# A second feed-forward product by seven half-block products on one Trainium2 core, with its sums kept on chip

## The chip, the cores and the metric

The kernel runs on one core of a Trainium2 chip. The metric is the device time of one execution in microseconds. TensorE (PE in the rows) multiplies into PSUM banks; VectorE (DVE), ScalarE (ACT) and GpSimd (POOL) work on tiles in SBUF and PSUM; SyncE (SP) issues most of the transfers. Each engine works through its own list in order and waits where an operand of an instruction isn't ready.

## The reference, cut to what matters

The program is one layer of a diffusion backbone. The change lies in its last part, the feed-forward block, for 128 context tokens and 1024 latent ones (1152 in all, nine tiles of 128; tile 0 is the context), with 1024 columns and 4096 hidden columns, in float32:

```python
u = layer_norm(x) * (1.0 + scale2) + shift2
hid = jnp.square(jax.nn.relu(u @ lw['w_fc'] + lw['b_fc']))
x = layer_norm(ALPHA * x + gate2 * (hid @ lw['w_proj'] + lw['b_proj']), lw['ln_g'][1], lw['ln_b'][1])
```

`gate2` is a row for the context tokens and one for the latent ones (`g2c`, `g2l` in the kernel); the kernel makes both from `w_ada` in `ada_rest`.

## The kernel before, in words

Every float32 operand is split into a high and a low part (`split`, L67 on ScalarE for the high part and L68 on VectorE or GpSimd for the low one), and each product is three matmuls (`mm3`, L111 to L113).

*First product* (`ffn1`, hidden = w_fc by u). The 4096 hidden columns are 16 pairs p of 128-column blocks. p = 0 and 1 are plain products. From p = 2 on each p is computed by Strassen's scheme in Winograd's form: a 2 by 2 split of the weights and of the tokens, seven products where the plain way has eight, with sums of weight parts (`prep`, tiles `S`) and of token parts (`sums`, tiles `Th` and `Tl`) made beforehand. A p is 14 steps (seven products, two token halves) of 12 matmuls 128x288. `need(n)` lets the preparation of weights run ahead. Each p ends with one store of its tile H (L1095), which VectorE has squared (L1260).

*Second product* (`ffn2`, hidden by w_proj) is plain. It runs over eight blocks b of four hidden tiles each, and in each over nine token tiles t: 24 matmuls 128x512 per tile, 1728 in all. VectorE adds each result onto `acc[t]` (L1341). `ahead(b + 1)` loads and splits the next block's hidden tiles (`lo`, `hi`) and weights (`ws`, `w`) meanwhile, and `ada_rest` makes the last columns of the gates between the tiles of blocks 0 to 5. In block 6 `residual(t)` multiplies by the gate (L1347, GpSimd) and adds ALPHA times `x2` (L1349, VectorE). In block 7 `stage_a` and `stage_c` finish each token tile: two halves of gate, addition and statistics on VectorE (L1378 to L1380), a small group (L1381, L130, L1384), normalising on ScalarE, `lng` and `lnb` on GpSimd (L1386, L1395). The last tile closes on VectorE (L1389, L1390).

## Time and profile before

| | |
|---|---|
| time, median of 3 runs | 2298.06 us (2292.59 to 2298.08) |
| the profiled execution, its own time | 2287.31 us |
| its span, first to last instruction | 2285.5 us |
| mean granted TensorE clock | 0.978 |
| PE busy | 94% of the span |
| DVE, ACT, POOL busy | 58%, 40%, 29% |

Busy shares are means over the whole span. A granted clock of 1.0 is TensorE's upper level (2.4 GHz), 0.5 the lower (1.2 GHz). A row of an instruction gives its start, its duration, its engine and line, what it writes and reads, and in brackets the engine's idle time before it and what ended that.

### The profile page before, as it was taken

The numbers are of one execution on the slowest core, as the hardware profiler recorded it, in microseconds if no ns is written. First come the engines' busy times: TensorE is split into PE (matmuls) and PEld (weight loads), VectorE is DVE, ScalarE is ACT, GpSimd is POOL, SyncE is SP. The second block draws the span as 40 slices with busy tenths as digits, with TensorE's granted clock in tenths as the row PEclk, the third lists the DMA queues.
The fourth block names the chain that finished last, engine by engine and source line by source line (L and its number), as shares of the span: only waits on it lengthen the run. The fifth ranks groups of instructions, "written<-read, shape, count | busy, mean of one in ns | idle before, by whom it ended". The sixth has DMA issues, their size and how long they took to land. (4 is left out here: it accounts for less than half of the span.)

```text
span 2285.5 us, 31722 instructions
## 1 busy us (share of the span) xinstructions
PE 2150.3 (94%) x12723; PEld 2021.9 (88%) x12723; DVE 1333.9 (58%) x2154; ACT 922.3 (40%) x1496; POOL 666.7 (29%) x367
## 2 busy tenths in 40 slices
PE   7988998999999899999999999969999979999996
PEld 4888998999999899999899998869999968888885
DVE  4464775676574555888734457764544436543378
ACT  5354424414424425787723224644444431121112
POOL 1402212412311312332302024353434302321176
PEclk9999999999999999999999999989999979999998
DMA  6121241133122121111432333442223253322442
GB/s 269 37 71 39 68 148 47 64 110 104 54 87 87 52 78 47 47 47 38 152 103 94 122 118 128 133 148 88 109 80 118 79 188 129 111 88 79 138 138 83
DMA packets 96755, 223.84 MB, mean 98 GB/s; under 512 B 20132, under 2 KB 48420, under 8 KB 93536
## 3 DMA queue, kind: packets, MB, share of 16 engines
q1 hardware_dynamic: 75008, 204.44, 26.5%
q10 hardware_dynamic: 21600, 17.38, 2.3%
q8 instruction: 99, 1.62, 0.3%
q14 instruction: 48, 0.39, 0.1%
HBM read 171.70 MB, written 50.09 MB: 97 GB/s over the span
## 5 line engine op out<-in xcount | busy, mean ns | idle before, releaser
L111 PE MATMUL pj<-hi,w 128*128 128x384 f32 (+1 forms) x2120 | 704.0, 332 | 22.4 <-ACT w L67 17.6
L112 PE MATMUL pj<-lo,w 128*128 128x384 f32 (+1 forms) x2120 | 701.2, 331 | 11.6 <-DVE lo L68 7.5
L113 PE MATMUL pj<-hi,w 128*128 128x384 f32 (+1 forms) x2120 | 700.8, 331 | 0.5 <-POOL w L68 0.5
L111 PEld LDWEIGHTS pj<-hi,w 128*128 128x128 f32 x2120 | 402.8, 190 | 24.5 <-ACT w L67 17.9
L112 PEld LDWEIGHTS pj<-lo,w 128*128 128x128 f32 x2120 | 402.7, 190 | 12.5 <-DVE lo L68 8.1
L113 PEld LDWEIGHTS pj<-hi,w 128*128 128x128 f32 x2120 | 402.3, 190 | 0.8 <-POOL w L68 0.8
L68 POOL TENSOR_TENSOR w<-ws,w 128x1024 fp32r<-128x1024 f32 (+1 forms) x91 | 187.5, 2064 | 559.1 <-ACT w L67 492.7
L67 ACT ACTIVATE w<-ws 128x1024 fp32r<-128x1024 f32 (+1 forms) x175 | 159.2, 915 | 384.8 <-DMA ws<-in_w_pr 241.3
L111 PE MATMUL pps<-w,hi 128*128 128x512 f32 x576 | 225.8, 392 | 15.4 <-ACT w L67 15.4
L112 PE MATMUL pps<-w,hi 128*128 128x512 f32 x576 | 226.0, 392 | 1.5 <-DVE w L68 1.5
L113 PE MATMUL pps<-w,lo 128*128 128x512 f32 x576 | 225.6, 392 | 0.0
L68 DVE TENSOR_TENSOR w<-ws,w 128x1024 fp32r<-128x1024 f32 (+1 forms) x84 | 104.9, 1255 | 107.3 <-ACT w L67 107.2
L1341 DVE TENSOR_TENSOR acc<-pps,acc 128x512 f32<-128x512 f32 x108 | 73.7, 691 | 146.6 <-PE pps L113 146.5
L111 PEld LDWEIGHTS pps<-w,hi 128*128 128x128 f32 x576 | 108.9, 189 | 39.4 <-ACT w L67 16.6
L111 PE MATMUL pj<-Th,w 128*128 128x288 f32 x448 | 132.7, 296 | 9.7 <-ACT e L1246 9.7
L113 PE MATMUL pj<-Th,w 128*128 128x288 f32 x448 | 132.0, 295 | 0.0
L112 PE MATMUL pj<-Tl,w 128*128 128x288 f32 x448 | 131.9, 294 | 0.0
L112 PEld LDWEIGHTS pps<-w,hi 128*128 128x128 f32 x576 | 109.0, 189 | 25.0 <-DVE w L68 2.4
L113 PEld LDWEIGHTS pps<-w,lo 128*128 128x128 f32 x576 | 109.1, 189 | 22.5
L716 POOL TENSOR_TENSOR CS<-Cst,CS 128x516 fp32r<-128x516 f32 x56 | 74.4, 1328 | 183.9 <-ACT CS L715 178.3
L464 POOL PARTITION_ALL_REDUCE aacc<-aacc x16 | 56.0, 3545 | 196.3 <-DVE aacc L463 170.3
L111 PEld LDWEIGHTS pj<-Th,w 128*128 128x128 f32 x448 | 84.0, 188 | 11.5 <-ACT e L1246 11.5
(313 smaller groups left out, 4055.1 us busy)
## 6 DMA issues: line engine op xcount, KB each, us to landing
ws<-in_w_in SPq DMA_DIRECT2D x56, 512.0 KB, 4.1
h<-Hf SPq DMA_DIRECT2D x16, 1152.0 KB, 5.1
lo<-h SPq DMA_DIRECT2D x32, 576.0 KB, 3.6
aw<-in_w_ada SPq DMA_DIRECT2D x64, 256.0 KB, 3.6
ws<-in_w_fc SPq DMA_DIRECT2D x32, 512.0 KB, 3.3
ws<-in_w_pr SPq DMA_DIRECT2D x32, 512.0 KB, 4.2
gm<-gs ACTq DMA_DIRECT2D x48, 192.0 KB, 1.9
gmr<-gm SPq DMA_DIRECT2D x16, 576.0 KB
```

The source lines that it names most:

```text
L67: self.nc.scalar.activation(hi, x, AF.Copy)
L68: (eng or self.nc.vector).tensor_tensor(lo, x, hi.bitcast(F), OP.subtract)
L111: mm(out, lhsT=ah, rhs=bh, start=first, stop=False, skip_group_check=onto)
L112: mm(out, lhsT=ah, rhs=bl, start=False, stop=False, skip_group_check=onto)
L113: mm(out, lhsT=al, rhs=bh, start=False, stop=last, skip_group_check=onto)
L464: nc.gpsimd.partition_all_reduce(acc[j], acc[j], channels=128, reduce_op=ReduceOp.add)
L716: nc.gpsimd.tensor_tensor(CS[d][1], Cst[d], CS[d][0].bitcast(F), OP.subtract)
L1341: nc.vector.tensor_tensor(acc[t][:, s], pss[n], (acc[t] if b else bp)[:, s], OP.add)
```

## The change

The second product is made by the same seven-product scheme for the eight latent tiles. Tokens and hidden columns are split in two; `KINDS` names the products by the weight part (B11, B21, B22) or sum of parts (T1 to T4) that they use. B12 is for the context alone, which stays plain. The hidden pairs fall in five blocks (`F2`) of 4, 4, 2, 4 and 2 pairs. Each product runs for four token slots j, 16 pairs by 4 slots by 7 products by 3 matmuls, 1344, and the context has 192: 1536 matmuls. Results per product are added up on chip in `Cj` and `Xj` over blocks 0 to 3; `combine` then puts them together at the end of block 3, with the gate and the residual (`residual`, L1501 and L1502). Block 4 adds its products on top in PSUM and finishes the tokens (`do`, `finish`, `norm`); before its first product `until(b, "B22")` issues all that is left of its preparation.

The hidden sums that the scheme needs are made in the first product. `store(p)` became a generator with four GpSimd sums of 512 columns and six transfers, which is run at the even steps of later p's. The token sums all come ahead of the first weight split, and `load(2)` stands a weight block earlier. The first product has 6 PSUM banks instead of 8. The last two columns of `ada_rest` move to the two branches of the mixer.

```diff
-            self.h_d = [self.dram.tile([128, 2, T], F, name=f"h{i}") for i in range(16)]
+            self.h_d = self.dram.tile([128, 7, 16, 512], F, name="h_d")
+            self.hc_d = self.dram.tile([128, 16, 2, 128], F, name="hc_d")
...
+        self.sides.append(self.ada_rest(p, range(6, 8), 1))
...
-        self.npj = 8
+        self.npj = 6
...
         def store(p, H):
-            nc.sync.dma_start(self.h_d[p], H)
...
+            a, b = (H[:, :, 128 + 512 * k:640 + 512 * k] for k in range(2))
+            to = lambda i, n=1: self.h_d[:, i:i + n, p, :]
+            t = lambda: pe.tile([128, 512], F, name="S", tag="S", bufs=5)
+            g = nc.gpsimd
+            s1, s2, s4 = t(), t(), t()
+            g.tensor_tensor(s1, b[:, 0], b[:, 1], OP.add)
             yield
...
+            g.tensor_tensor(s2, s1, a[:, 0], OP.subtract)
+            nc.sync.dma_start(self.hc_d[:, p], H[:, :, 0:128])
+            nc.sync.dma_start(to(0, 2), a)
+            yield
+            g.tensor_tensor(b[:, 0], a[:, 0], b[:, 0], OP.subtract)
+            nc.sync.dma_start(to(4)[:, 0], s1)
+            yield
+            g.tensor_tensor(s4, a[:, 1], s2, OP.subtract)
+            nc.sync.dma_start(to(5)[:, 0], s2)
+            yield
+            nc.sync.dma_start(to(2, 2), b)
+            yield
+            nc.sync.dma_start(to(6)[:, 0], s4)
+            yield
...
+                if p and i:
+                    load(2)
...
+                    if p and i:
+                        need(c)
...
+                self.f2_start()
+            if i in (6, 9, 12):
+                self.f2_ahead(i // 3 - 2)
...
+                elif stores and next(stores[0], stores) is stores:
+                    stores.pop(0)
...
+    F2 = [(0, 4), (4, 4), (8, 2), (10, 4), (14, 2)]
+    KINDS = ["B11", "B12", "T1", "T2", "T3", "B21", "T4", "B22"]
+    ROW = {"B11": 0, "T1": 4, "T2": 5, "T3": 2, "B21": 1, "T4": 3, "B22": 6}
...
+        def ahead():
+            for b in range(NB):
+                g = self.F2[b][1]
+                load_raw(b)
+                self.f2_load(b, None)
+                split = [lambda i=i: self.f2_split(b, None, i) for i in range(2)]
+                for kind in self.KINDS:
+                    n = H_KINDS.index(kind) if kind != "B12" else None
+                    if n is not None and (b or n):
+                        while not unit_free(b, n):
+                            yield
+                        if b or n > 1:
+                            self.f2_load(b, n)
+                        split += [lambda i=i: self.f2_split(b, n, i, g_ if i or kind in ("T1", "T2") else v) for i in range(2)]
+                    for i in range(g // 2):
+                        if (b, kind, i) not in self.wts:
+                            own = b == NB - 1 and kind in ("B21", "T4", "B22")
+                            while (own and "w" not in late) or (not own and tiles[0] >= tiles[1] + 5):
+                                yield
+                            self.w2, self.nw2 = (late["w"], 3) if own else (pw if tiles[0] % 5 == 4 else None, 1)
+                            tiles[0] += not own
+                            self.f2_weight(b, kind, [source(b, kind, 2 * i + j) for j in range(2)], i, [g_, v])
+                            yield
+                    while split:
+                        split.pop(0)()
+                        yield
+                    done.add((b, kind))
+        work = ahead()
...
+        def until(b, kind):
+            n = 0
+            while (b, kind) not in done:
+                next(work, None)
+                n += 1
+                assert n < 100
...
+        acc = {"B11": lambda j: Xj[j][:, 0], "T1": lambda j: Cj[j][:, 3], "T2": lambda j: Xj[j][:, 1],
+               "T3": lambda j: Xj[j][:, 2], "B21": lambda j: Cj[j][:, 0], "T4": lambda j: Cj[j][:, 2],
+               "B22": lambda j: Cj[j][:, 1]}
+        half = {"T1": 1, "B21": 0, "T4": 0}
...
+        def residual(t):
+            y = tile_of(t)
+            x2 = big("x2", ("r21", "r30", "r31")[t % 3])
+            nc.sync.dma_start(x2, self.x2_d[t])
+            g_.tensor_tensor(y, y, rows["g2l" if t else "g2c"], OP.mult)
+            v.scalar_tensor_tensor(y, x2, ALPHA, y, OP.mult, OP.add)
...
+        def combine(kind):
+            for j in range(4):
+                C, X = Cj[j], Xj[j]
+                add = lambda e, o, x: e.tensor_tensor(o, o, x, OP.add)
+                if kind == "T2":
+                    add(v, X[:, 1], X[:, 0])
+                elif kind == "T3":
+                    add(g_, X[:, 2], X[:, 1])
+                    add(g_, X[:, 1], C[:, 3])
+                    add(v, C[:, 3], X[:, 2])
+                elif kind == "B21":
+                    add(g_, C[:, 0], X[:, 0])
+                elif kind == "T4":
+                    add(g_, C[:, 2], X[:, 2])
+                    residual(5 + j)
+                elif kind == "B22":
+                    add(v, C[:, 1], X[:, 1])
...
+        for b in range(NB - 1):
+            for q, kind in enumerate(self.KINDS):
+                until(b, kind)
+                if kind in ("B11", "B12", "B21", "B22"):
...
+                if kind != "B12":
+                    for j in range(4):
+                        ps = bank()
+                        product(b, kind, j, ps)
+                        o = acc[kind](j)
+                        if b:
+                            v.tensor_tensor(o, ps, o, OP.add)
...
+                    used.add(7 * b + H_KINDS.index(kind))
+                tiles[1] += self.F2[b][1] // 2
+                if b == NB - 2:
+                    if kind == "T3":
+                        row("g2l", "r20", self.mod_d[3][1])
+                        row("g2c", "bp", self.mod_d[3][0])
+                    combine(kind)
+                    if kind == "B22":
+                        residual(0)
+        px.close()
+        late["w"] = self.pool(st, "w3")
+        b = NB - 1
+        until(b, "B22")
+        row("lng", "r00", I["ln_g"][1:2, :])
+        row("lnb", "r01", I["ln_b"][1:2, :])
...
+        def keep(i, j):
+            if i == 1:
+                x = big("e", ("r21", "r30")[j % 2])
+                ev[1, j], ev[2, j] = x[:, 0:512], x[:, 512:D]
+            elif i == 3:
+                x = big("e", ("r31", "r10")[j % 2])
+                ev[3, j], ev[4, j] = x[:, 0:512], x[:, 512:D]
+            nc.scalar.activation(ev[i, j], A[j], AF.Copy)
...
+        def do(P, j):
+            if P == 1:
+                A[j] = bank()
+                product(b, "B11", j, A[j])
+                keep(1, j)
+            elif P == 5:
...
+            elif P == 6:
+                product(b, "T2", j, A[j], False)
+                keep(2, j)
+            elif P == 7:
+                product(b, "T3", j, A[j], False)
+                keep(3, j)
...
+                t = ev[4, j]
+                v.tensor_tensor(t, Cb[j], ev[3, j], OP.add)
+                v.tensor_tensor(t, t, rows["g2l"][:, 512:D], OP.mult)
+                y = tile_of(5 + j)[:, 512:D]
+                v.tensor_tensor(y, y, t, OP.add)
...
+            elif P == 4:
+                product(b, "T4", j, A[j], False)
+                finish(5 + j, 0, A[j])
...
+        seq = [(1, 0), (5, 0), (6, 0)]
+        for j in range(4):
+            n = j + 1
+            seq += [(1, n), (7, j), (5, n), (2, j), (4, j), (3, j), (6, n)] if n < 4 else \
+                   ["B11", (7, j), "B12", (2, j), (4, j), (3, j), "B21", "B22"]
+        for x in seq:
```

SP's order between the two products, before: the last store of H, the bias row, two weights, four hidden tiles.

```order
L1095 DMA h_119<-Hf 128x2304 [waits DMAHW7_49,DVE_49]
L1310 DMA bp<-in_b_pr 128x1024 [waits DMAHW0_49,PE_49]
L1296 DMA ws<-in_w_pr 128x1024 [waits DMAHW5_49,DMAHW1_49]
L1296 DMA ws<-in_w_pr 128x1024 [waits DMAHW6_49,DMAHW2_49]
L1287 DMA lo<-h_106 128x1152 [waits DMAHW3_49,PE_49]
L1287 DMA lo<-h_106 128x1152 [waits DMAHW4_49,PE_49]
L1287 DMA lo<-h_107 128x1152 [waits PE_49] x2
```

After: the last sum's store, the bias row, the eight weights of block 0 (`raw`), then the context's tile (`hc_d`) and the next product's tokens. 

```order
L1119 DMA h_d<-S 128x512 [waits DMAHW5_49,Pool_49]
L1524 DMA bp<-in_b_pr 128x1024 [waits DMAHW6_49,PE_49]
L1387 DMA raw<-in_w_pr 128x1024 [waits DMAHW7_49]
L1387 DMA raw<-in_w_pr 128x1024 [waits DMAHW0_49]
L1387 DMA raw<-in_w_pr 128x1024 [waits DMAHW1_49]
L1387 DMA raw<-in_w_pr 128x1024 [waits DMAHW2_49]
L1387 DMA raw<-in_w_pr 128x1024 [waits DMAHW3_49]
L1387 DMA raw<-in_w_pr 128x1024 [waits DMAHW4_49]
L1387 DMA raw<-in_w_pr 128x1024 [waits DMAHW5_49]
L1387 DMA raw<-in_w_pr 128x1024 [waits DMAHW6_49]
L1332 DMA lo<-hc_d 128x1024 [waits DMAHW7_49,PE_49]
L1335 DMA lo<-h_d 128x2048 [waits DMAHW0_49]
```

The first product's own tokens and half weights stand further up, but what the first matmuls (the context's) need has moved behind the stores of the sums and all eight weights.

GpSimd's order at the end of block 6, before: gate multiplications (L1347) and splits of the next block's weights, then the first tokens' `lng` (L1386).

```order
L68 TENSOR_TENSOR w<-ws,w 128x1024 [waits DMAHW0_49,Activation_49]
L1347 TENSOR_TENSOR acc_17279<-acc_17279,g2l 128x1024 [waits DVE_49]
L1347 TENSOR_TENSOR acc_17280<-acc_17280,g2l 128x1024 [waits DVE_49]
L68 TENSOR_TENSOR w<-ws,w 128x1024 [waits DMAHW3_49,Activation_49]
L1347 TENSOR_TENSOR acc_17281<-acc_17281,g2l 128x1024 [waits DVE_49]
L1347 TENSOR_TENSOR acc_17282<-acc_17282,g2l 128x1024 [waits DVE_49]
L1386 TENSOR_TENSOR acc_17274<-acc_17274,lng 128x1024 [waits Activation_49]
L1386 TENSOR_TENSOR acc_17275<-acc_17275,lng 128x1024 [waits Activation_49]
```

After, at the end of block 3: the four multiplications of `combine("B22")` (L1501) and the context's, then the first of the instructions that prepare block 4 (L68 splits, L1397 and L1399 differences of weights).

```order
L1501 TENSOR_TENSOR C_17536<-C_17536,g2l 128x1024 [waits DVE_49]
L1501 TENSOR_TENSOR C_17537<-C_17537,g2l 128x1024 [waits DVE_49]
L1501 TENSOR_TENSOR C_17538<-C_17538,g2l 128x1024 [waits DVE_49]
L1501 TENSOR_TENSOR C_17539<-C_17539,g2l 128x1024 [waits DVE_49]
L1501 TENSOR_TENSOR ctx<-ctx,g2c 128x1024 [waits DMAHW1_49]
L68 TENSOR_TENSOR w<-raw,w 128x512 [waits Activation_49] x2
L68 TENSOR_TENSOR lo<-lo,hi 128x512 [waits DMAHW2_49,Activation_49]
L68 TENSOR_TENSOR lo<-lo,hi 128x512 [waits Activation_49]
L68 TENSOR_TENSOR w<-raw,w 128x512 [waits Activation_49]
L68 TENSOR_TENSOR lo<-lo,hi 128x512 [waits DMAHW3_49,Activation_49]
L68 TENSOR_TENSOR lo<-lo,hi 128x512 [waits Activation_49]
L1397 TENSOR_TENSOR raw<-raw 128x512 [waits DMAHW4_49,Pool_49]
```

The multiplications no longer alternate with splits: they stand in one piece, each waiting for VectorE, and the 19 instructions of block 4's preparation have moved behind them.

VectorE's order in block 6, before: evictions (L1341) and residuals (L1349).

```order
L1341 TENSOR_TENSOR acc_17276<-pps,acc_17276 128x512 [waits PE_49] x2
L68 TENSOR_TENSOR lo<-lo,hi 128x1152 [waits DMAHW5_49,Activation_49]
L1349 SCALAR_TENSOR_TENSOR acc_17275<-x_19166,acc_17275 128x1024 [waits DMAHW3_49,Pool_49]
L1341 TENSOR_TENSOR acc_17277<-pps,acc_17277 128x512 [waits PE_49] x2
L1349 SCALAR_TENSOR_TENSOR acc_17276<-x_19200,acc_17276 128x1024 [waits DMAHW4_49,Pool_49]
L1341 TENSOR_TENSOR acc_17278<-pps,acc_17278 128x512 [waits PE_49] x2
L68 TENSOR_TENSOR lo<-lo,hi 128x1152 [waits DMAHW6_49,Activation_49]
L1349 SCALAR_TENSOR_TENSOR acc_17277<-x_19237,acc_17277 128x1024 [waits DMAHW6_49,Pool_49]
L1341 TENSOR_TENSOR acc_17279<-pps,acc_17279 128x512 [waits PE_49] x2
L1349 SCALAR_TENSOR_TENSOR acc_17278<-x_19271,acc_17278 128x1024 [waits DMAHW7_49,Pool_49]
```

After, behind the last eviction of block 3: additions (L1508) and residuals (L1502), then block 4's weights.

```order
L1508 TENSOR_TENSOR C_17536<-C_17536,X_17551 128x512 [waits DVE_49]
L1502 SCALAR_TENSOR_TENSOR C_17536<-x_19744,C_17536 128x1024 [waits DMAHW5_49,Pool_49]
L1508 TENSOR_TENSOR C_17537<-C_17537,X_17552 128x512
L1502 SCALAR_TENSOR_TENSOR C_17537<-x_19749,C_17537 128x1024 [waits DMAHW6_49,Pool_49]
L1508 TENSOR_TENSOR C_17538<-C_17538,X_17553 128x512
L1502 SCALAR_TENSOR_TENSOR C_17538<-x_19754,C_17538 128x1024 [waits DMAHW7_49,Pool_49]
L1508 TENSOR_TENSOR C_17539<-C_17539,X_17554 128x512
L1502 SCALAR_TENSOR_TENSOR C_17539<-x_19759,C_17539 128x1024 [waits DMAHW0_49,Pool_49]
L1502 SCALAR_TENSOR_TENSOR ctx<-x_19763,ctx 128x1024 [waits DMAHW1_49,Pool_49]
L68 TENSOR_TENSOR w<-raw,w 128x512 [waits Activation_49]
L1393 TENSOR_TENSOR raw<-raw 128x512 x2
```

Between two residuals there stood the evictions of another tile; now there stands the addition for which the next multiplication waits, and each residual waits for that multiplication. Block 4's preparation follows here too.

ScalarE's order around the first copy of block 4's accumulator (L1567), after; the kernel before has no such copy and ends its splits in block 6.

```order
L67 ACTIVATE hi<-lo 128x512 [waits DMAHW6_49,Activation_49]
L67 ACTIVATE hi<-lo 128x512
L67 ACTIVATE w<-raw 128x512 x2
L67 ACTIVATE hi<-lo 128x512 [waits DMAHW7_49,Activation_49]
L67 ACTIVATE hi<-lo 128x512
L1567 ACTIVATE e<-pps 128x512 [waits DMAHW1_49,PE_49]
L1567 ACTIVATE e<-pps 128x512 [waits PE_49]
```

The first copy stands behind the last of ScalarE's splits for block 4.

## Rows read from the trace of the kernel before

**Rows 1.** Part 1 of the page: busy us (share of the span), instructions.

```profile
PE 2150.3 (94%) x12723; PEld 2021.9 (88%) x12723; DVE 1333.9 (58%) x2154; ACT 922.3 (40%) x1496; POOL 666.7 (29%) x367
```

**Rows 2.** Stretches: length, then busy (count) of PE, PEld, DVE, ACT, POOL; clock, DMA share, GB/s.

```profile
1260.00:1340.00 80.00, 80.00 (x463) 80.00 (x462) 36.89 (x54) 19.56 (x19) 0.00 (x0) 1.00 0.35 124
1600.00:1850.00 250.00, 244.91 (x1843) 243.76 (x1842) 109.50 (x137) 106.40 (x226) 92.72 (x62) 1.00 0.29 107
1853.50:1882.00 28.50, 11.52 (x30) 7.86 (x29) 11.88 (x13) 7.17 (x9) 0.00 (x0) 0.58 0.58 213
1872.00:1880.00 8.00, 4.89 (x11) 3.55 (x12) 2.73 (x3) 2.11 (x2) 0.00 (x0) 0.50 1.02 414
1882.00:2218.60 336.60, 336.60 (x1486) 278.69 (x1485) 171.94 (x193) 58.80 (x56) 115.66 (x40) 1.00 0.35 115
2218.60:2267.50 48.90, 48.90 (x216) 40.19 (x215) 44.67 (x71) 10.78 (x14) 29.95 (x14) 1.00 0.14 56
2267.50:2285.50 18.00, 0.05 (x1) 0.00 (x0) 13.90 (x19) 1.83 (x3) 11.76 (x5) 0.59 0.32 127
```

**Rows 3.** All engines in order of start, after the last matmul.

```profile
2269.51 2.35 POOL L1395 TENSOR_TENSOR acc<-acc,lnb 128x1024 f32<-128x1024 f32 x1
2269.99 0.21 DVE L1381 BATCH_NORM_AGGREGATE mv<-st 128x2 f32<-128x12 f32 x1
...
2270.82 1.05 DVE L1384 SCALAR_TENSOR_TENSOR mv<-mv 128x1 f32<-128x1 f32 x1
2271.80 0.69 DVE L1378 TENSOR_TENSOR pps<-pps,g2l 128x512 f32<-128x512 f32 x1
...
2276.02 0.21 DVE L1381 BATCH_NORM_AGGREGATE mv<-st 128x2 f32<-128x12 f32 x1
...
2276.73 1.69 DVE L1389 SCALAR_TENSOR_TENSOR acc<-acc,mv,lng 128x512 f32<-128x512 f32 x1
```

**Rows 4.** Groups by shape, 1600 to 1850 us: count, busy us, mean ns, idle before.

```profile
L68 POOL TENSOR_TENSOR w<-S,w 128x512 fp32r<-128x512 f32 x31 | 49.3, 1598 | 41.0 <-ACT w L67 40.6
L68 POOL TENSOR_TENSOR w<-ws,w 128x512 fp32r<-128x512 f32 x31 | 43.7, 1408 | 105.1 <-ACT w L67 105.1
...
L1183 DVE TENSOR_TENSOR S<-ws 128x512 f32<-128x512 f32 x10 | 16.8, 1681 | 0.8 <-DMA ws<-in_w_fc 0.8
...
L1186 DVE TENSOR_TENSOR S<-S,ws 128x512 f32<-128x512 f32 x10 | 6.9, 693 | 0.9
```

**Rows 5.** Groups by shape from 1882 us to the end.

```profile
L1347 POOL TENSOR_TENSOR acc<-acc,g2l 128x1024 f32<-128x1024 f32 x8 | 27.3, 3416 | 3.8 <-DVE acc L1341 3.8
...
L1349 DVE SCALAR_TENSOR_TENSOR acc<-x,acc 128x1024 f32<-128x1024 f32 x9 | 23.3, 2594 | 0.0
...
L1379 DVE TENSOR_TENSOR acc<-acc,pps 128x512 f32<-128x512 f32 x18 | 12.4, 688 | 0.6
...
L1347 POOL TENSOR_TENSOR acc<-acc,g2c 128x1024 f32<-128x1024 f32 x1 | 2.4, 2398 | 33.2 <-DMA x<-x 33.2
```

**Rows 6.** All engines in order of start, where the first product's Strassen part begins.

```profile
1526.32 0.63 ACT L67 ACTIVATE w<-ws 128x512 fp32r<-128x512 f32 x1 [5.87 <-DMA ws<-in_w_fc]
...
1527.00 0.61 PE L111 MATMUL pj<-hi,w 128*128 128x288 f32 x1 [17.58 <-ACT w L67]
1527.03 1.26 POOL L68 TENSOR_TENSOR w<-ws,w 128x512 fp32r<-128x512 f32 x1 [6.04 <-ACT w L67]
```

**Rows 7.** All engines in order of start, from the second product's first matmul on.

```profile
1853.58 0.39 PE L111 MATMUL pps<-w,hi 128*128 128x512 f32 x1
...
1863.14 1.36 DVE L1260 TENSOR_TENSOR Hf<-Hf 128x1152 f32<-128x1152 f32 x1 [0.60 <-ACT Hf L1092]
...
1874.64 0.80 PE L111 MATMUL pps<-w,hi 128*128 128x512 f32 x1 [13.70 <-ACT w L67]
...
1876.49 0.63 PE L113 MATMUL pps<-w,lo 128*128 128x512 f32 x1
...
1881.79 0.40 PE L111 MATMUL pps<-w,hi 128*128 128x512 f32 x1
```

More of the change, by code (lines that the diff above doesn't have):

```diff
@@ L454, in ada_rest @@
                 yield
-                if k in (1, 3) and late:
+                while late and (k > 2 or bufs == 1):
                     late.pop(0)()
+                if k == 0:
+                    acc = [p.tile([128, 512], F, name="aacc", tag=f"aacc{j}", bufs=bufs) for j in range(2)]
                 for j in range(2):
@@ L962, in branches @@
         wo[7] = self.w_next(("out", 7), 0)
+        assert not self.sides
         sm.close()
@@ L1098, in ffn1, with need @@
+        weights = prep()
+        def need(n):
+            while len(ready) < n and next(weights, 0) is None:
+                pass
         Hs = [new_h() for _ in range(2)]
@@ new lines, in ffn2, with load_raw @@
+        ctx = p.tile([128, D], F, name="ctx")
+        rp = self.pool(st, "raw")
+        big = lambda n, tag: rp.tile([128, D], F, name=n, tag=tag)
+        bp = big("bp", "bp")
+        NB = len(self.F2)
+        raws = {}
+        def load_raw(b):
+            k0, g = self.F2[b]
+            for k in range(g):
+                raws[b, k] = [big("raw", f"r{k}{i}") for i in range(2)]
+                for i in range(2):
+                    nc.sync.dma_start(raws[b, k][i], I["w_pr"][2 * (k0 + k) + i])
```

362 lines of the change are left out of this document (198 added, 164 removed).

## The prediction

> **What bounds the kernel now.** I read the busy totals of the page first, then windows around the two feed-forward products, then the single instructions where TensorE (PE) stops. The reader should see in [rows 1] that PE is busy 94% of the span and VectorE (DVE) 58%, and in [rows 2] that this average has three parts. In the body of the first product PE works 244.91 of 250 us. In the first seven blocks of the second it works without a gap. At its start (1853.5 to 1882) PE is busy only 11.52 of 28.5 us at a granted clock of 0.58, and after the last matmul DVE alone runs on. The last block gives the price of a 128x512 matmul: 216 in 48.90 us, so 0.2264 us each. Seven blocks hold 1512 of them, 342.3 us; they take from 1853.58 [rows 7] to 2218.6, 365.0 us. So 22.7 us are lost at the start: the chain of H store, loads and splits, a wait of 13.70 us, then matmuls at half the clock (13 from 1876.49 to 1881.79, 0.41 each) [rows 7]. From 2218.6 to the end of the span it is 66.9 us, with DVE 44.67 of 48.90 busy [rows 2]: the tail is near DVE's limit already.
>
> **The change part by part.** The sum is made against the profiled execution (2287.3 us: the span of 2285.5 and 1.8 around it), 10.8 under the median shown (2298.06); the total is then added to the median.
>
> *PE work.* 192 of 1728 matmuls go: 43.5 us. Of the 1536 that remain, 1344 lie in blocks 0 to 3 (1176 latent, 168 context), 168 fewer than before's 1512, so −38.0 up to that place. The other 192 fall in the tail, which DVE and POOL set, so they come in there.
>
> *First product, start.* ScalarE's first weight split there waits 5.87 us for weights [rows 6], behind the token sums, which keep their engines. Loads issued a weight block earlier remove this: −5.9 (bounds 0, and −17.6, the whole idle time [rows 6]). *ada_rest* moves under the branches, where PE stays at 80.00 of 80 us and POOL at nothing [rows 2]: 0; without that cover its four POOL reductions would show.
>
> *First product, body.* Each p adds four POOL sums of 512 columns, at 1.4 to 1.6 us [rows 4] some 6.0 us. A p lasts 168/1843 of 250 us, 22.8; POOL goes from 92.7/250 (8.5 us) to 14.5 of 22.8. PE's surplus hides it, but DVE's first write of a new H now waits for the last sum and a store of the p two before, and PE has 6 banks for 8. Bounds 0 and +14 (a microsecond per p); I take +3.
>
> *Start of the second product.* SP's fence is the path: eight raw weights and the context tile, which the first matmuls need, stand behind the last store of POOL's sums. The last square ended at 1863.14+1.36, 10.9 us after 1853.58 [rows 7]; half of the splits ahead of it have gone to POOL, so I estimate 7. Four sums at 1.5 follow, SP is free at 13; bp, eight raws and the context are ten transfers of 0.52 MB, 12.7 us at 414 GB/s [rows 2]; about 2 to land and 1.5 for splits make 29. With half-clock matmuls (13×0.18=2.4) the loss is 32 against 22.7: +9 (bounds +4, +16). Here no matmul runs before the wait.
>
> *Blocks 0 to 3.* T1's second weight tile takes the place of B11's first, so it waits for PE to be done with that. Behind it POOL has half a weight tile (1.4 [rows 4]) and two token splits of 1024 columns (2.40 each [rows 5]); with ScalarE's split ahead that is 7 to 8 us. PE has 18 matmuls (the context's 12 and T1's first 6) to fill them, 4.1 us. That leaves about 4 us in each of three four-pair blocks, +12 (0 to +16). Before block 3 the raws again stand behind a token unit that waits for T3's end: 5.2 MB plus splits, about 16 us, against 19 of PE work; +5 (0 to +20) since any lateness of POOL adds to it.
>
> *The tail.* I count from t, the last matmul of block 3 (before: 2218.6, and 66.9 us). POOL's fence is what matters. First, four rounds of DVE addition, POOL multiplication, DVE combination, each waiting for the one before: 0.69 + 2.40 [rows 5] + 1.4 (twice the 693 ns of 512 columns [rows 4]) + 0.2 for hand-overs, 4.7 each. POOL ends the fourth and the context's at 0.7 + 3×4.7 + 3.1 + 2.4 = t+20. With the contended prices (3.42 and 2.59 [rows 5]) it is t+28. Then 19 operations of 512 columns prepare block 4, between 1.26 alone [rows 6] and 1.60 [rows 4], with 1.5: t+48.5 (24 to 30 us for them). ScalarE's first copy of block 4's accumulator (L1567) stands behind its own splits, which pace with POOL's: T2's matmuls, which add onto that accumulator, cannot begin before. Copy, 18 matmuls, two more copies: 4.1 to 7.4 + 1.9, so DVE begins its tail at t+55.
>
> DVE then has per token slot 15 large operations at 0.70 (six from 2271.80 to 2276.02) and two small groups at 1.81 (2269.99 to 2271.80) [rows 3]: 14.1, four slots 56.5. Context: six large, 4.2, a small group 0.7 (2276.02 to 2276.73), and 8.8 from the first closing operation (2276.73) to the end of the span (2285.5). That makes 70.2, and t+125. PE's 42 matmuls per slot, 9.5 us, hide below 14.1. Against 66.9: **+58** (lower bound: POOL at 1.26, DVE from t+50 on with small groups of 0.7, 61, so +44; upper: t+28, 30 of preparation and 9 to DVE's start, t+67, and 8 DVE operations 1.0 longer, 78, so +78).
>
> Here is the place for a rule. POOL's L1395 ends at 2271.86 and DVE's 128x1 operation beside it, begun at 2270.82, at 2271.87; DVE's difference of two SBUF tiles takes 1681 ns beside POOL where the same size takes 693 [rows 3, 4]. The Trainium skill (SBUF — State Buffer, Who interferes with whom) says that a DVE instruction with two SBUF inputs and a GpSimd instruction that reads SBUF block each other for the whole instruction; the trace agrees in these places. By that rule DVE's 15 operations of block 4's preparation add themselves to POOL's 19: 10.4 + 24 = 34 us in place of 28.5, and the sum would be 6 larger.
>
> **Sum:** −38.0 − 5.9 + 3 + 9 + 12 + 5 + 58 = **+43**: 2330 for an execution like the profiled one, and 2298 + 43 = **2341** on the median.
>
> **The rivals.**
> *Faster: block 4's preparation overlaps.* Without the tail the terms make −15, so the kernel is faster when the tail ends before t+82. DVE alone needs 70, so it would have to begin by t+12. For it: DVE is busy 171.94 and ScalarE 58.80 of 336.60 us in blocks 1 to 6 [rows 2], so there is room, and the first accumulators of block 4 could be filled early. Against it: POOL's order puts the 19 operations behind a chain that can't begin before t. If it began at t+5 the end is t+75, and −15+8 gives 2291; without T1's stalls too, 2279. Chance 0.07.
> *No change.* Every lower bound at once is −38 −17.6 +4 +44 = −8, so 2290; with the 17.6 at its forecast of 5.9 it is +4, 2302. What lies between is no change. Chance 0.05.
> *Slower still: POOL and DVE in each other's way.* By the pair 1681 against 693 each of DVE's two-tile operations beside POOL costs 1.0 more: with eight in the tail (L1614, L1616) +8, +6 in the preparation, and the first product at its upper bound, 11 over my 3. That is 2341+25=2366. For it: POOL gets four operations more in each p, and 19 beside DVE's 15 before the tail. Against it: DVE's operations with one input in PSUM, most of the tail, keep 688 ns beside POOL (L1379) [rows 5]. Chance 0.15.
>
> **How the numbers follow.** My forecast has 0.73, the rivals 0.07, 0.05, 0.15. The forecast's own terms leave about ±25 around 2341; the range reaches down to 2303, where several lower bounds meet, and up to 2385, past the contended case with late loads. A measurement of this kernel tells about 0.3% (7 us) from no change. Faster 0.07, same 0.05, slower 0.88.
>
> **What would show it.** In the profile after: PE idle about 29 us (22 to 39) between the two products, with SP's loads behind the last sum's store; short waits of PE for POOL's splits in T1; and from the end of block 3 some 50 us in which POOL is busy nearly throughout and PE nearly idle, then DVE nearly gapless for 70 us. The first product's body should keep its 22.8 us per p, and its start lose about 6 us of its idle time. The prediction is wrong if PE runs block 4's products right after block 3, or if DVE's stalls on H stop PE in the first product.

## The result, and the profile after

The changed kernel takes **2395.0 us** (2393.28 to 2396.57, four runs) against 2298.07 (2292.59 to 2301.13, four runs): ratio **1.0424** [1.0403, 1.0445]. It is slower, as forecast, but by 97 us where I had put 43, and 10 us above the end of my range.

Page part 1 of the changed kernel, to be read against [rows 1]:

```profile
PE 2138.6 (89%) x12531; PEld 2000.2 (84%) x12531; DVE 1432.7 (60%) x2251; ACT 1000.5 (42%) x1668; POOL 934.3 (39%) x560
```

PE lost the 192 matmuls, but only 11.7 us of its 2150.3, since more of the others run slower. POOL gained 268 us. Windows of the changed kernel (columns as in [rows 2]): the first product's Strassen part; from its last matmul to the second product's first; blocks 0 to 3; from t, the last matmul of block 3, to DVE's first closing operation; the rest. (By this t, 2244.7, two matmuls of block 4's context, begun before the next pause, are counted in: 0.4 us.)

```profile
1535.40:1868.90 333.50, 317.98 (x2352) 314.97 (x2352) 152.27 (x182) 137.55 (x297) 205.63 (x142) 0.99 0.40 136
1868.90:1903.50 34.60, 0.03 (x1) 0.00 (x0) 6.47 (x4) 3.40 (x8) 16.30 (x11) 0.53 0.73 273
1903.50:2244.70 341.20, 320.41 (x1346) 256.13 (x1346) 207.81 (x219) 124.59 (x193) 230.83 (x136) 0.97 0.33 119
2244.70:2313.40 68.70, 13.57 (x33) 9.07 (x33) 37.19 (x34) 15.50 (x28) 47.17 (x28) 0.53 0.28 99
2313.40:2394.80 81.40, 42.76 (x160) 33.57 (x158) 56.24 (x96) 16.81 (x26) 37.55 (x16) 0.76 0.15 58
```

The spans differ by 2394.8 − 2285.5 = 109.3, more than the medians do, because the profiled execution of before lies 10.8 under its median. Four stretches make it up:

| stretch | before | after | change | forecast |
|---|---|---|---|---|
| start to the first Strassen matmul | 1527.0 | 1535.5 | +8.5 | −5.9 |
| first product, Strassen part | 326.6 | 333.4 | +6.8 | +3 |
| its end to t | 365.0 | 375.8 | +10.8 | −12 |
| t to the end of the span | 66.9 | 150.1 | +83.2 | +58 |

Of the +8.5, 10.3 stand already at one matmul at the start of the mixer's branches (1137.99 and 1148.27 us from the start of their spans). The kernels run later have the changed kernel's code up to there and put the same matmul at 1140.1 to 1145.8, so executions of the same code differ by up to 8 us at this place. The kernel before differs ahead of it only in the step at which `ada_rest` stores its columns, and one execution of it was profiled; whether that step adds to the 10.3 stays open.

**From the first product to t.** PE's longest waits from 1868 us to the end, then the order at the fence on POOL and on SP's queue, of the changed kernel:

```profile
PE pps L111 <- ACT hi L67: 65.1, 6, 34.6
PE pps L111 <- ACT e L1567: 40.5, 4, 19.8
PE pps L113 <- DVE lo L68: 14.1, 5, 11.6
PE pps L113 <- POOL lo L68: 11.5, 12, 1.9
```

```profile
1873.87 1.71 POOL L1105 TENSOR_TENSOR S<-Hf 128x512 f32<-128x512 f32 x1
...
1884.09 1.26 POOL L1114 TENSOR_TENSOR S<-Hf,S 128x512 f32<-128x512 f32 x1
...
1885.38 0.32 SPq L1119 DMA_DIRECT2D h_d<-S  x1
1885.79 0.41 SPq L1524 DMA_DIRECT2D bp<-in_b_pr  x1
1886.25 5.33 SPq L1387 DMA_DIRECT2D raw<-in_w_pr  x8
1892.61 0.33 SPq L1332 DMA_DIRECT2D lo<-hc_d  x1
...
1903.54 0.79 PE L111 MATMUL pps<-w,hi 128*128 128x512 f32 x1 [34.62 <-ACT hi L67]
```

From the first to the last POOL row there are eight sums, those of p = 14 and of p = 15; their last store leaves SP at 1885.38, and the context tile that the first matmul needs comes behind it and behind eight weights. From 1903.5 to t, 1346 matmuls would take 304.7 us at 0.2264 each (from [rows 2]). PE is busy 320.4 and idle 20.8, so gap and stretch lose 34.6 + 15.7 + 20.8 = 71.1 where before lost 22.7. Of the 15.7, some 8 to 9 lie at 41 matmuls that take more than 0.51 us, most of them behind the longest waits and most of them 0.63 us long, with 0.43 from one to the next (as behind 2215.44); the rest lies in matmuls just before and after the short waits (0.33 to 0.4 from one to the next).

**From t to the end.** DVE and POOL around t, then ScalarE, PE and DVE where the closing part begins and where its first slot ends (changed kernel, in order of start for each engine):

```profile
2250.35 2.27 DVE L1502 SCALAR_TENSOR_TENSOR C<-x,C 128x1024 f32<-128x1024 f32 x1 [2.23 <-POOL C L1501]
...
2256.21 0.68 DVE L1536 TENSOR_TENSOR C<-pps,C 128x512 f32<-128x512 f32 x1
2256.81 0.68 DVE L1508 TENSOR_TENSOR C<-C,X 128x512 f32<-128x512 f32 x1
2259.94 1.23 DVE L1502 SCALAR_TENSOR_TENSOR C<-x,C 128x1024 f32<-128x1024 f32 x1 [2.46 <-POOL C L1501]
...
2257.56 2.35 POOL L1501 TENSOR_TENSOR C<-C,g2l 128x1024 f32<-128x1024 f32 x1 [6.02 <-DVE C L1508]
2261.85 2.34 POOL L1501 TENSOR_TENSOR C<-C,g2l 128x1024 f32<-128x1024 f32 x1 [1.94 <-DVE C L1508]
...
2272.70 2.34 POOL L1501 TENSOR_TENSOR ctx<-ctx,g2c 128x1024 f32<-128x1024 f32 x1
...
2280.35 1.27 POOL L68 TENSOR_TENSOR w<-raw,w 128x512 fp32r<-128x512 f32 x1 [3.10 <-ACT w L67]
...
2306.42 1.72 POOL L68 TENSOR_TENSOR lo<-lo,hi 128x512 fp32r<-128x512 f32 x1
```

```profile
2279.64 1.15 ACT L67 ACTIVATE w<-raw 128x512 fp32r<-128x512 f32 x2 [47.21 <-DVE raw L1393]
...
2304.96 0.57 ACT L1567 ACTIVATE e<-pps 128x512 f32<-128x512 f32 x1
...
2325.81 1.24 ACT L144 ACTIVATE C<-C,mv 128x1024 f32<-128x1024 f32 x1 [0.42 <-DVE mv L1591]
2326.96 1.06 ACT L1567 ACTIVATE e<-pps 128x512 f32<-128x512 f32 x2
...
2327.59 0.80 PE L111 MATMUL pps<-w,hi 128*128 128x512 f32 x1 [6.65 <-ACT e L1567]
...
2313.44 0.69 DVE L1613 TENSOR_TENSOR e<-pps,e 128x512 f32<-128x512 f32 x1 [6.44 <-ACT e L1567]
...
2331.18 0.69 DVE L1613 TENSOR_TENSOR e<-pps,e 128x512 f32<-128x512 f32 x1 [5.41 <-ACT e L1567]
```

Block 3's last evictions (L1536) are queued on DVE behind T4's four residuals (L1502), each of which waits for a gate on POOL (L1501). So B22's chain begins at 2256.8, t+12, and POOL is done with the gates at 2275.0, t+30. Its preparation of block 4 takes until 2308.1: 33.1 us, of which its 19 operations fill 28.8. The longest wait in it (3.10) is for ScalarE's split of T1's weights, and that waits for VectorE's difference of them (L1393), queued behind two residuals. ScalarE's first copy of an accumulator (L1567) comes at 2304.96, and DVE begins at t+68.7. A slot then takes 17.7 to 18.7 us (L1613 at 2313.44, 2331.18, 2349.76, 2368.42), because ScalarE makes the next slot's copy behind normalising (L144), for which it waits for DVE, and PE and then DVE wait for that copy.

### The profile page after: what moved, and what is told of

Its sections match the earlier page's. It is cut to its first block, busy times and chain, and to the rows that moved or that the text cites. A ratio compares the mean times of both kernels' runs of the same rounds, so it can differ in the third digit from the quotient of the medians.

```text
span 2394.8 us, 32091 instructions
## 1 busy us (share of the span) xinstructions
PE 2138.6 (89%) x12531; PEld 2000.2 (84%) x12531; DVE 1432.7 (60%) x2251; ACT 1000.5 (42%) x1668; POOL 934.3 (39%) x560
## 5 line engine op out<-in xcount | busy, mean ns | idle before, releaser
L111 PE MATMUL pps<-w,hi 128*128 128x512 f32 x512 | 208.7, 408 | 105.5 <-ACT hi L67 65.1
L68 POOL TENSOR_TENSOR w<-ws,w 128x512 fp32r<-128x512 f32 (+1 forms) x65 | 115.0, 1770 | 320.1 <-ACT w L67 311.9
L113 PE MATMUL pps<-w,lo 128*128 128x512 f32 x512 | 209.0, 408 | 25.6 <-DVE lo L68 14.1
L111 PEld LDWEIGHTS pps<-w,hi 128*128 128x128 f32 x512 | 100.7, 197 | 130.5 <-ACT hi L67 68.1
L112 PE MATMUL pps<-w,hi 128*128 128x512 f32 x512 | 206.7, 404 | 0.0
L67 ACT ACTIVATE w<-raw 128x512 fp32r<-128x512 f32 x124 | 73.5, 625 | 222.5 <-DVE raw L1393 53.4
L68 DVE TENSOR_TENSOR w<-ws,w 128x1024 fp32r<-128x1024 f32 (+1 forms) x82 | 104.1, 1275 | 100.3 <-ACT w L67 100.3
L67 ACT ACTIVATE w<-ws 128x1024 fp32r<-128x1024 f32 (+1 forms) x147 | 127.4, 874 | 49.7 <-PE pj L113 36.9
L113 PEld LDWEIGHTS pps<-w,lo 128*128 128x128 f32 x512 | 100.4, 196 | 57.2 <-POOL lo L68 18.8
L68 POOL TENSOR_TENSOR lo<-lo,hi 128x1024 fp32r<-128x1024 f32 (+2 forms) x48 | 111.3, 2329 | 47.2 <-ACT hi L67 47.0
L68 POOL TENSOR_TENSOR w<-raw,w 128x512 fp32r<-128x512 f32 x62 | 92.1, 1489 | 95.4 <-ACT w L67 95.4
```

The costliest lines, as they stand in the source:

```text
L67: self.nc.scalar.activation(hi, x, AF.Copy)
L68: (eng or self.nc.vector).tensor_tensor(lo, x, hi.bitcast(F), OP.subtract)
L111: mm(out, lhsT=ah, rhs=bh, start=first, stop=False, skip_group_check=onto)
L112: mm(out, lhsT=ah, rhs=bl, start=False, stop=False, skip_group_check=onto)
L113: mm(out, lhsT=al, rhs=bh, start=False, stop=last, skip_group_check=onto)
```

## The experiments

The kernel before, run beside them, had medians of 2291.2 to 2292.4, some 6 us less than in the first comparison; so ratios are compared, not medians. An execution is also compared from its first Strassen matmul to its end (758.5 before, 859.3 changed), which leaves out the stage that moves by itself. These are single executions: from the first product's end to t, where the changed kernel and three of the runs (product by product, T2 ahead, normalising later) have the same code, they took 372.5 to 377.1 us, so a difference of 4 us in that comparison can be chance. Where an edit acts behind t, t to the end (150.1 in the changed kernel) is compared. Their times stand in one table behind the first three.

**Start of the preparation.** Block 4's weights and splits are issued product by product, as each is first used:

```
-        until(b, "B22")
...
         def do(P, j):
+            until(b, {1: "B11", 5: "T1", 6: "T2", 7: "T3", 2: "B21"}.get(P, "B22"))
```

> Block 4's preparation is no longer issued in one piece ahead of its products; each product issues its own just before it. Theory (the order holds the tail up: ScalarE's first copy of the accumulator stands behind all splits of block 4): that copy comes some 20 us sooner after the last matmul of block 3 (60 us in the changed kernel), VectorE's closing operations begin some 20 us sooner, and the kernel is 10 to 25 us faster than the changed one. Rival (GpSimd's and VectorE's work in the tail fills the time in any order): the copy comes sooner, but the end moves by less than 4 us.

ScalarE's first copy came at t+34.5 instead of t+60.2 and DVE's first closing operation at t+53 instead of t+68.7. But its first slot took 27.0 us (2291.63 to 2318.65), for the splits now lie between its products, and t to the end became 144.0 instead of 150.1. The start of DVE's work was therefore late by the preparation, as the theory says; but most of what it wins is work that has still to be done, and the gain of 6 us lies between the theory's 10 to 25 and the rival's 4.

**T2 of the next slot ahead of T4 and B22:**

```
-            seq += [(1, n), (7, j), (5, n), (2, j), (4, j), (3, j), (6, n)] if n < 4 else \
+            seq += [(1, n), (7, j), (5, n), (2, j), (6, n), (4, j), (3, j)] if n < 4 else \
```

> In the tail T2's product of the next token slot is issued ahead of T4's and B22's of this one, so that its copy on ScalarE stands ahead of the normalising. Theory (VectorE waits 5.4 us in each of three slots because the copy stands behind ScalarE's normalising, which waits for VectorE): a slot takes 13 to 15 us where it takes 18.3, and the kernel is 10 to 16 us faster than the changed one. Rival (the slot is set by GpSimd's four multiplications and additions and by half-clock matmuls): slots stay above 17 us, less than 4 us gained.

DVE's wait for the copy fell from 5.41 to 2.28 us, yet after a first slot of 14.6 the next two took 18.2 and 18.1. Two of the three copies still stand behind normalising, and two DVE operations came to lie beside POOL's `lng` and `lnb`. The small gain (1.1 us from t to the end) is the rival's; its reason isn't, since the slots fall to 14.9 below with GpSimd's work as it is, once all three copies move. DVE and POOL of this kernel in its second slot:

```profile
2319.43 0.69 DVE L1613 TENSOR_TENSOR e<-pps,e 128x512 f32<-128x512 f32 x1 [2.28 <-ACT e L1567]
2319.52 2.37 POOL L1593 TENSOR_TENSOR C<-C,lng 128x1024 f32<-128x1024 f32 x1
2320.16 2.28 DVE L1614 TENSOR_TENSOR e<-e,g2l 128x512 f32<-128x512 f32 x1
2321.96 2.72 POOL L1594 TENSOR_TENSOR C<-C,lnb 128x1024 f32<-128x1024 f32 x1
2322.47 2.76 DVE L1616 TENSOR_TENSOR C<-C,e 128x512 f32<-128x512 f32 x1
```

**The context tile ahead of the eight weights** in the queue:

```
-                load_raw(b)
                 self.f2_load(b, None)
+                load_raw(b)
```

> The context's hidden tile is loaded ahead of the eight raw weights of a block, not behind them. Theory (the first matmuls of the second product wait for the transfer behind 4.2 MB): PE's idle time between the products falls from 34.6 to about 26 us, the kernel is 6 to 9 us faster. Rival (B12's weights from the same raws are late next, or the clock stays low for longer): the gap falls, but another wait in block 0 gives back more than half of it, 0 to 4 us gained.

The gap between the products fell from 34.62 to 23.72 us, and the time by a little more. The mechanism of the theory holds, with more than the 6 to 9 us that it named: the place of one small load behind 4 MB cost about 11 us.

| kernel | us (runs) | ratio | Strassen to end | against the changed kernel |
|---|---|---|---|---|
| product by product | 2383.4 (2) | 1.0395 [1.0364, 1.0427] | 854.0 | −5.3 |
| T2 ahead | 2388.2 (2) | 1.0417 [1.0383, 1.0450] | 855.9 | −3.4 |
| context first | 2379.0 (2) | 1.0376 [1.0346, 1.0407] | 845.8 | −13.5 |
| no sums | 2384.5 (2) | 1.0401 [1.0367, 1.0435] | 853.2 | −6.1 |
| chain in rows | 2388.6 (2) | 1.0419 [1.0394, 1.0444] | 854.4 | −4.9 |
| normalising later | 2377.5 (2) | 1.0371 [1.0343, 1.0399] | 847.0 | −12.3 |
| four edits | 2362.8 (4) | 1.0307 [1.0287, 1.0328] | 834.4 | −24.9 |
| `ada_rest` moved, alone | 2297.7 (10) | 1.0023 [1.0012, 1.0034] | – | – |
| last block plain | 2299.4 (7) | 1.0035 [1.0022, 1.0049] | 771.2 | −88.1 |
| additions behind preparation | 2301.9 (5) | 1.0042 [1.0030, 1.0054] | 769.7 | −89.6 |
| T1's split on DVE too | 2299.1 (7) | 1.0025 [1.0014, 1.0036] | 767.4 | −91.9 |

**The four POOL sums** of each p left out:

```
-            g.tensor_tensor(s1, b[:, 0], b[:, 1], OP.add)
+            s1 = s2 = s4 = self.zero
...
-            g.tensor_tensor(s2, s1, a[:, 0], OP.subtract)
...
-            g.tensor_tensor(b[:, 0], a[:, 0], b[:, 0], OP.subtract)
...
-            g.tensor_tensor(s4, a[:, 1], s2, OP.subtract)
```

> The four GpSimd sums per pair are left out, and zeros are stored in their place (the hidden sums are missing from the second product). Theory (the sums cost twice: in the first product's body and, eight of them in a row, ahead of SP's loads): the body from the first Strassen matmul to the last goes back from 333 to about 327 us, PE's idle time between the products from 34.6 to about 25 us; 13 to 17 us faster in all. Rival (the stores' traffic and the in-order queue cost, not the sums): the body stays within 2 us of 333.

The body stayed at 333.0, so the sums' POOL time is not what lengthened it, which is the rival's side. What stands there instead is one late store. The first of these rows of the changed kernel is DVE's first write of the last H, the others are PE's two longest waits in the second half of the body:

```profile
1860.94 0.46 DVE L1277 TENSOR_TENSOR Hf<-pj,e 128x288 f32<-128x288 f32 x1 [14.99 <-DMA h_d<-Hf]
...
1861.46 0.40 PE L111 MATMUL pj<-hi,w 128*128 128x288 f32 x1 [2.17 <-DVE Hf L1277]
...
1865.46 0.40 PE L111 MATMUL pj<-Th,w 128*128 128x288 f32 x1 [2.15 <-ACT e L1268]
```

DVE waits for the store of the H two before, and PE then waits 2.17 us for DVE and 2.15 for ScalarE behind it. In the last-block-plain kernel below, which has the body at 328.3, both waits are gone; that the loads issued ahead for the second product are what holds up the store is argued from the order on SP, and wasn't tried alone. The gap between the products fell by 4.4 us (34.62 to 30.17), half of what I expected. Without the sums, five stores, the bias row and the eight weights still stand on SP between VectorE's last square and the context's load, which leaves 11.3 us behind that square instead of 15.8 (1880.33 − 1868.99 against 1892.61 − 1876.80).

**The chain of gates without waits**: the four additions first, then POOL's gates one behind another, and all residuals last on DVE:

```
-                    residual(1 + j)
+                    gate(1 + j)
...
-                        residual(0)
+                        gate(0)
+                        residuals()
```

> At the end of block 3 all four additions of B22 come first on VectorE, GpSimd's nine gate multiplications follow without a wait between them, and VectorE's nine residuals come last. Theory (VectorE's evictions of B22 are held by T4's residuals, and each of B22's multiplications then waits for a residual): GpSimd is through with the multiplications about 18 us after the last matmul of block 3 where it is 30 in the changed kernel, and everything behind comes as much sooner: 9 to 13 us faster than the changed kernel. Rival (what stands behind waits for transfers or VectorE, not GpSimd): GpSimd is free sooner, less than 4 us gained.

The gates no longer waited, and POOL was through them at t+23 instead of t+30. It then stood still: T1's weight differences (L1393 here) were queued on DVE behind nine residuals (L1511). DVE and POOL of this kernel:

```profile
2246.03 12.62 POOL L1506 TENSOR_TENSOR C<-C,g2l 128x1024 f32<-128x1024 f32 x4
2246.54 16.48 DVE L1511 SCALAR_TENSOR_TENSOR C<-x,C 128x1024 f32<-128x1024 f32 x5
2258.61 3.32 POOL L1506 TENSOR_TENSOR ctx<-ctx,g2c 128x1024 f32<-128x1024 f32 x1
...
2270.84 1.29 DVE L1393 TENSOR_TENSOR raw<-raw 128x512 f32<-128x512 f32 x2
...
2272.35 1.27 POOL L68 TENSOR_TENSOR w<-raw,w 128x512 fp32r<-128x512 f32 x1 [8.21 <-ACT w L67]
```

POOL waits 8.21 us and t to the end is 147.1 (−3.0): the rival. The first two rows also give the price of the overlap. A gate takes 3.2 us (12.62 / 4) and a residual 3.3 (16.48 / 5) beside one another, where they take 2.34 and 1.23 one after the other (L1501, L1502 above). Both together take about 3.3 instead of 3.6, so running them at the same time saves next to nothing.

**Normalising behind the next slot's copies:**

```
                 v.tensor_tensor(y, y, t, OP.add)
+                flush()
...
-                norm(5 + j)
+                pend.append(5 + j)
...
-                norm(1 + j)
+                pend.append(1 + j)
```

> In the tail the normalising of a slot's two tiles is issued behind the next slot's copies, not ahead of them; nothing else moves. Theory (all three copies of the next slot, not T2's alone, stand behind a normalising that waits for VectorE): PE's waits of 6.6 us for a copy and VectorE's of 5.4 us in three slots nearly go, a slot takes 14 to 15.5 us instead of 18.3; 9 to 13 us faster than the changed kernel. Rival (VectorE's and GpSimd's work sets the slot): slots above 17 us, less than 4 us gained.

The first closing operations of the four slots, of this kernel:

```profile
2300.55 0.69 DVE L1619 TENSOR_TENSOR e<-pps,e 128x512 f32<-128x512 f32 x1 [5.81 <-ACT e L1567]
...
2310.87 0.67 DVE L1619 TENSOR_TENSOR e<-pps,e 128x512 f32<-128x512 f32 x1
...
2325.74 0.68 DVE L1619 TENSOR_TENSOR e<-pps,e 128x512 f32<-128x512 f32 x1
...
2340.57 0.67 DVE L1619 TENSOR_TENSOR e<-pps,e 128x512 f32<-128x512 f32 x1
```

The waits ahead of the later slots are gone, and a slot takes 14.9 us (the first 10.3, without small groups). The theory holds, and 14.1 was a fair price of DVE's own work in a slot (it is busy 13.3 in the second). Of the 15.0 us that the three slots gain, 8.7 reach t to the end (141.4): what follows the last slot's first closing operation grows from 26.4 to 32.6, as the small groups and normalising left over stand there.

**Four edits together** (product by product, context first, chain in rows, normalising later):

> Four edits together: the context's tile ahead of the raws, block 4's preparation issued product by product, additions first at the end of block 3, normalising behind the next slot's copies. Theory (each removes a wait of its own on the path): about 11 + 5 + 11 + 11, so 35 to 45 us faster than the changed kernel, 2350 to 2360, still 2 to 3% slower than before. Rival (they remove the same wait, since GpSimd's work in the tail, some 80 us with the normalising, becomes the bound): 20 to 28 us.

The ratio falls from 1.0424 to 1.0307, 27 us, and the stretch from the first Strassen matmul on by 24.9. (The medians differ by 32, but the kernel before was 6 faster beside it, too.) The number lies in the rival's range, but its reason, that the edits remove the same wait, is not what the stretches show: the single edits gave 10.9 in the gap and 6.1, 3.0 and 8.7 from t to the end, 28.7 together, and the four at once give 11.1 and 16.1. The theory's 38 was too much mainly because it took 11 for the chain, which gave 3. t to the end is 134.0 us, still twice that of before.

**`ada_rest` moved, alone in the kernel before:**

```
+        self.sides.append(self.ada_rest(p, range(6, 8), 1))
         for br in range(2):
```

> The kernel before, with one part of the change alone: the last two columns of ada_rest under the branches. Theory (the branch stage of the changed kernel and of four variants takes 327.7 to 329.3 us where before took 325.8, by this part): the branch stage takes 328 to 329 us, and the kernel is 0 to 3 us slower than before. Rival (the stage differs from execution to execution): the stage stays within 1 us of 325.8.

Slower by 0.2%, 5 us (3 to 8); the branches take 328.5 us against 325.8. So the stage grows as the theory says, but the time by more than its 0 to 3, and where the rest lies stays open. No matmul moves with the edit: the stage has 1688 in both kernels, and what comes to it are 36 operations on VectorE and four reductions on GpSimd (L465, 3.3 to 3.6 us each). PE's waits in the stage, first of the kernel before, then of this one (the 4.0 at the first matmul of the stage are in both):

```profile
PE pj L112 <- DVE lo L68: 7.5, 2, 4.0
...
PE pj L112 <- DVE lo L68: 8.5, 2, 4.5
...
PE pj L112 <- POOL lo L68: 2.4, 4, 1.6
```

PE waits 1.0 us longer for a split on VectorE and 2.4 us for splits on GpSimd, for which it didn't wait before. Which of the moved operations makes those splits late wasn't followed.

**The last block plain**: no Strassen products in block 4, so 24 matmuls for each of eight latent tiles and the context's; its preparation ahead of B22's additions; no hidden sums for the last two p; the context first and the gates in a row, as above.

```
-                for kind in self.KINDS:
+                for kind in self.KINDS if b < NB - 1 else PLAIN:
...
+                    if kind == "B22":
+                        until(NB - 1, "B22")
                     combine(kind)
...
-            stores.append(store(p, H))
+            if p < 14:
+                stores.append(store(p, H))
```

> The last block (pairs 14 and 15) is computed plainly, 24 matmuls per token tile as before the change, and its preparation is issued ahead of B22's additions; its hidden sums aren't made, so eight GpSimd sums no longer stand ahead of SP's loads between the products. The context is loaded ahead of the raws, and the gate multiplications at the end of block 3 follow without a wait between them. The first four blocks keep the seven products. Theory (the tail, not the seven-product scheme in the body, lost the time: block 4's sums and splits and 15 operations per slot on VectorE): from the last matmul of block 3 to the end 80 to 95 us instead of 150, PE's idle time between the products under 22 us; 2305 to 2325 in all, 70 to 90 us faster than the changed kernel and 0.5 to 1.5% slower than before. Rival (the combination of the seven products at the end of block 3 keeps GpSimd and VectorE busy whatever follows): the last stretch stays above 115 us, 2335 or more.

The ratio falls from 1.0424 to 1.0035, so 89 us of the loss come back: the theory, at its upper end. By stretches, 5.1 of it lie in the body, 19.5 in the gap and 64.4 behind t (to the same matmul in both). Several edits act together here: the 48 us between this tail and that of the four edits can't be divided between the plain products and the preparation that is issued ahead of B22's additions. Windows of this kernel (body, gap, blocks 0 to 3, t to the end; columns as in [rows 2]):

```profile
1529.30:1857.60 328.30, 317.26 (x2352) 314.91 (x2352) 156.50 (x183) 139.97 (x301) 208.45 (x143) 0.99 0.40 140
1857.60:1872.70 15.10, 0.07 (x1) 0.00 (x0) 4.72 (x4) 1.20 (x4) 2.42 (x2) 0.64 0.61 210
1872.70:2215.40 342.70, 324.01 (x1348) 260.07 (x1348) 212.56 (x226) 130.30 (x204) 229.66 (x137) 0.95 0.36 134
2215.40:2300.60 85.20, 52.66 (x212) 42.00 (x212) 76.57 (x103) 12.62 (x17) 68.29 (x30) 0.83 0.30 105
```

What still keeps it from being faster shows here. Gap and blocks together are 357.8 against 365.0 of before, where 168 matmuls less should give 38: PE is idle 15.1 + 18.7 us and loses 18.8 in slower matmuls (324.0 − 305.2 for 1348), 61 of them longer than 0.51 us. That leaves −7.2, against +18.3 from t to the end.

**Two attempts on those waits.** Preparation ahead of T3's additions and of T4's gates, and then T1's first token split on DVE as well:

```
-                    if kind == "B22":
-                        until(NB - 1, "B22")
+                    if kind in ("T3", "T4", "B22"):
+                        until(*{"T3": (b, "T4"), "T4": (NB - 1, "B12"), "B22": (NB - 1, "B22")}[kind])
```

> The kernel with the plain last block, and in block 3 the preparation of T4 is issued ahead of GpSimd's additions for T3, that of the last block's first two weight parts ahead of the gate multiplications of T4. Theory (GpSimd's and VectorE's order at the end of block 3 still stops PE: 5.5 us ahead of T4's product, 7.8 and 1.9 at the start of the last block, each followed by matmuls at half the clock): those waits nearly go, 8 to 14 us faster than the kernel with the plain last block, 2286 to 2292, level with before or up to 0.3% faster. Rival (VectorE's and GpSimd's work is only moved, and the last stretch grows by what the waits lose): within 4 us of 2299.

```
-                        split += [lambda i=i: self.f2_split(b, n, i, g_ if i or kind in ("T1", "T2") else v) for i in range(2)]
+                        split += [lambda i=i: self.f2_split(b, n, i, g_ if i or kind == "T2" else v) for i in range(2)]
```

> As the one before, and the first half of T1's tokens is split on VectorE, not on GpSimd. Theory (T1's second weight tile and its token splits stand in a row on GpSimd behind B11's end): PE's waits of some 4 us in T1 of blocks 0, 1 and 3 fall to 2 or less, 4 to 8 us faster than the one before. Rival (VectorE's split takes as long beside GpSimd, since both have two inputs in SBUF): less than 2 us.

The first moved the waits and didn't shorten them, as its rival says. PE of that kernel at its two longest waits behind the gap, the second of them in the last block:

```profile
2191.79 0.79 PE L111 MATMUL pps<-w,hi 128*128 128x512 f32 x1 [6.97 <-DVE C L1553]
...
2230.70 0.79 PE L112 MATMUL pps<-w,hi 128*128 128x512 f32 x1 [14.11 <-POOL w L68]
```

The second took T1's waits for POOL from 1.9 us to 1.0 at most, though PE's short waits only change engine (for POOL's token splits 9.6 to 6.9 us, for DVE's 1.1 to 5.1), and 3.6 us from the stretch between the gap and the pause behind block 3 (344.3 to 340.7). In time it is 2 to 4 us: between theory and rival, and within the noise of the two ratios. No version beats the kernel before.

## Why the prediction was right in sign and wrong in size

**The tail: the step that failed.** "0.7 + 3×4.7 + 3.1 + 2.4 = t+20" let B22's chain begin at t. The four residuals of T4, which I had not counted, are queued ahead of the last evictions on DVE and wait for POOL's gates: the chain began at t+12 and ended at t+30. My price of a round (4.7) was rather high, 4.28 measured. The preparation took 33.1 us (2275.0 to 2308.1) instead of 28.5: its operations fill 28.8, as I had them, and what I left out are 4.3 us in which POOL waits for ScalarE, 3.1 of them again behind operations queued on DVE. DVE began at t+68.7 instead of t+55. The second half, "PE's 42 matmuls per slot, 9.5 us, hide below 14.1", left out ScalarE: its copies stand behind normalising, which waits for DVE. So a slot was 18.3 and DVE's part 81.4 instead of 70.2. Together this is +25 on the +58.

By the rule of the Trainium skill (SBUF — State Buffer, Who interferes with whom), that a DVE instruction with two SBUF inputs and a GpSimd instruction that reads SBUF contend, my estimate for the preparation was 34 us, with DVE's operations added to POOL's. The measured 33.1 looks like it, but isn't: POOL's operations fill 28.8 of it and the rest are waits for ScalarE. The rule shows in single operations, POOL's of 512 columns at 1.7 us beside DVE's and 1.26 alone, and the 3.2 and 3.3 us of gate and residual side by side nearly agree with it. (GpSimd's rows here all read and write SBUF; none has a tile in PSUM.)

**Start of the second product, +9.** The mechanism, SP's fence behind POOL's sums, was right. The idle time was 34.6 instead of 29, since eight sums stood there and not "four sums at 1.5".

**Blocks 0 to 3, +12 and +5.** PE's idle time of 20.8 us is near the 17. Its makeup is not: T1's waits came to about 9, block 2 to 3 to about 2, and 5.5 stand at 2215.44, for T4's weights behind eight additions of T3 on POOL that I hadn't counted. What I left out are the slower matmuls at those waits, 15.7 us in all, where I had 2.4 behind the first one. With the six above this makes +23 on the −12.

**First product.** Start −5.9: PE's idle time there [rows 6] fell from 17.58 to 12.36, −5.2, right. Body +3: it was +6.8, and not from the sums; 4.3 of it are the two waits at the last H, one of them the stall of DVE on H that I had named as a sign of being wrong. `ada_rest` at nothing was wrong by 3 us in the branches: I took one window of 80 us in which POOL does nothing [rows 2] for the whole stage, and PE now waits for splits on DVE and POOL in other parts of it.

**The rivals.** "POOL and DVE in each other's way" (2366) is the nearest, and part of it is real (L1614 at 2.28 and L1616 at 2.76 in the second experiment), but it doesn't hold the misses above: most are operations waiting in line behind others that wait. The errors by stretch, 3 + 4 + 23 + 25 (the first without the 10.3 ahead of the branches), sum to 55, and 43 + 55 = 98 is near the measured 97.

## What to carry to other kernels

Before a chain that crosses two engines is priced from the moment its data exist, list everything that is queued ahead of it on each engine, with what that waits for: here four earlier operations with their own waits cost 12 us, and a copy behind a normalisation 3 to 4 us in a slot. A scheme that spares TensorE work can pay only where TensorE is the bound, and here its waits took most of that too: of 38 us of matmuls, the kernel with the plain last block kept 7 from the end of the first product to t. At the end of the kernel, where the other engines finish, seven products with their sums took 134 us from t even with their chain mended, and the plain eight 85. And waits of TensorE cost more than their length, by the slower matmuls around them.

## What I had not expected of the hardware

- A multiplication on POOL and a two-input operation on DVE, both from SBUF, take 3.2 and 3.3 us side by side, and 2.34 and 1.23 one after the other: overlap gains a tenth.
- Behind a wait of TensorE of 5.51 us (at 2215.44) stand 15 matmuls of 0.5 to 0.8 us, most of 0.63, and the granted clock from 2215.4 to 2232 is 0.77; before had no matmul over 0.4 us in blocks 1 to 6. With the slower matmuls at short waits this took 16 us that no list of waits shows.
- The same matmul, with the same code ahead of it, began between 1140 and 1148 us from the start in twelve profiled executions, so a single profile can't show a change of a few us behind it; stretches counted from a matmul further on can.
